# Two-dimensional neighbourhood attention layer: query blocks paired anew so that four bias tables serve in place of six, the final root by logarithm and exponential on ACT, and the last head pair of every row group split without a round trip through memory

## The chip, the cores and the metric

The kernel runs on one core of one Trainium2 chip. A core has five engines with queues of their own: TensorE (PE, matrix products, with PEld for its weight loads), VectorE (DVE), ScalarE (ACT), GpSimd (POOL) and SyncE (SP, which here issues nearly all DMAs). The metric is the time of one execution in microseconds (us), less is better; several runs are taken and their median is compared.

## What is computed

One layer over 2048 tokens of 1024 features, laid out as a grid of 32 rows by 64 columns, all in float32. A root-mean-square norm, a projection to q, k, v and a gate (4 x 1024 columns), attention with 16 heads of 64 features, an output projection with the input added, and a final norm:

```python
h = rmsnorm(x, norm_0)
q, k, v, gate = split(h @ w_in_0, 4)
# query (r, c): keys in a window of 8 rows by 16 columns, moved inward at the border
s = q . k * 64 ** -0.5 + rpb[head, kr - r + 7, kc - c + 15]      # outside the window: -1e30
o = softmax(s) @ v
x = x + (o * silu(gate)) @ w_out_0
return rmsnorm(x, norm_f)            # x * rsqrt(mean(x * x) + 1e-6) * norm_f
```

## The kernel before

**Three stages.** `stage_one` and `stage_two` do the projections, for each half of the tokens, by a scheme of seven products of half-size blocks, each in three float32r products of high and low parts (h·h, h·l, l·h; `split_to` makes the parts: ACT copies to the rounded type, DVE subtracts). Their results q, k, v and the gate go to memory. The third stage, the loop over `m` at L1281, does the attention and, between its pieces, the rest of the value projection (`values_left`, 192 matmuls) and then the output projection (`outputs`, 768 matmuls); these matmuls are called the fill here.

**Attention steps.** `order` has 32 steps: four row groups T of eight grid rows, and in each eight head pairs p. A step has 512 queries, by columns eight strips of 8 columns by 8 rows, that is 64 queries a strip. A strip sees the keys of three strips, its own and the two beside it, over 11, 15, 15 or 12 key rows by row group. Two strips share the 128 partitions of a block; a block C in 0 to 3 held strips 2C and 2C+1.

- `scores` (L916): q times k into PSUM (line 929, tile s), then DVE adds the table `EM` and takes the minimum over a row (L937), and ACT makes the exponential with its sum (L943). Tables hold the bias and -1e30 outside the window, so they depend on the row group, the head, and on where the block stands: first, middle (blocks 1 and 2) or last, so three kinds by two heads, six tables. `load_tab` (L902) loads them for a step, into two buffers `em`.
- `normalise` (L946): DVE takes the reciprocal of the four sums of half a step (L948), and POOL multiplies the four tiles (L952). The second half of a step is normalised in the next turn of the loop.
- `turns` (L954): TensorE transposes the weights, strip by strip, into PSUM (ph, L968); ACT copies those of the lower 64 partitions and DVE those of the upper 64 to SBUF (pta, L971), in three rounds.
- `values` (L974): the weights times v (o, L986), times the gate (DVE, og, L990). The result goes to memory (`keep`, L992), to be loaded by row tiles of 128 tokens (`load_og`).

**The output part.** There are 16 row tiles n, four in a row group; tile n needs all eight head pairs of its row group, 128 columns (a slot) each. `load_og` loads the slots (ograw, L1043), `split_og` makes the high and low parts (ACT L1056 gh, DVE L1057 gl), and 24 matmuls for each half j of the columns (L1210, L1212, L1214, tile po) make a turn. `turns_` lists the turns. In row groups 0 and 3 the last head pair's result is also split directly (`direct`, L997, into the tile `last`), so that the first two row tiles of these groups load only seven slots; `parts`, `whole` and `og_ready` say what must be there. `add_rows` adds the input (DVE, L1089) and squares with a sum (ACT, L1092). `finish` queues the root: eight small DVE instructions (L1106 to L1113, a first guess from the bits and two steps of refinement), then the scaling (`scale`, L1121, two of 128x512 on DVE), then the store (`send`, L1125). For the last tile the root is a square root on ACT (L1103), whose activation table is loaded by an early square root (L1081), and a reciprocal on DVE.

**What sets the order.** The order is written by hand. All is issued in program order on each engine. `clock` counts the matmuls of the fill; `store` keeps a piece of work until the clock has reached a due time (`due`). `now` is the clock with 26 added for each step. A turn of the loop is: `feed(10)` (ten matmuls), `normalise` of the second half of the step before, then four portions of fill, each with a `split_rows` or a load of weights (`consume`) ahead of it, `run_roots` behind the second portion, the last 0.3 of the amount (with up to `calm_debt` = 6 matmuls in advance where something was added or split within 8 counts), then `turns`, `scores` of the next step with the first half's `normalise` in it, and `values`. About 24 matmuls of fill stand in a step. `split_rows` splits a tile that was loaded 40 counts ago, whole, and at most three turns away. A root is run at the earliest 8 counts behind its tile's last addition; its scaling comes 9 counts behind the root and its store 27. SP issues the DMAs of a step in this order: the store of og, then v, q, the table, the keys, the gate, with row tiles, inputs, weights and stores of output in between.

## Time and profile before

| | before |
|---|---|
| median of 3 runs | 1052.13 us (1048.69 to 1052.44) |
| the profiled execution, its own time | 1049.58 us |
| its span | 1047.8 us |
| granted TensorE clock | 0.998 |
| busy: PE, PEld, DVE, ACT, POOL | 1033.4, 819.7, 706.6, 482.2, 214.4 us |
| DMA | 200.25 MB, mean 191 GB/s |
| the attention stage, from its first fill to the last matmul | 598.7 to 1041.6 us |

The span is what the profile covers, from its first to its last instruction. PE's busy time is modelled and includes short waits. Rows of groups give the line, the engine, the operation, out<-in with shapes, the count, then busy us, mean ns of one, idle us ahead and what ended it. Rows of the timeline and of the chain begin with the start and the length in us. In brackets stands the idle time ahead of an instruction and what ended it.

### The profile page before, as it was taken

How to read it: one execution, taken by the hardware profiler on the slowest of the kernel's cores; microseconds unless marked ns; L12 is line 12 of the kernel's file. 1: busy time of each engine (PE TensorE's matmuls, PEld its weight loads, DVE VectorE, ACT ScalarE, POOL GpSimd, SP SyncE). 2: the span in 40 equal slices, each digit the busy share in tenths (PEclk: the TensorE clock that was granted, in tenths of full speed). 3: DMA queues.
4: the chain of work that ended last, by engine and by line, in shares of the span. 5: the costliest groups of instructions: out<-in, count | busy, mean ns of one | idle time of the engine just before them, and what ended most of it. 6: DMA issues, size and time to landing. Idle time of an engine off the chain costs nothing.

```text
span 1047.8 us, 19452 instructions
## 1 busy us (share of the span) xinstructions
PE 1033.4 (99%) x7024; PEld 819.7 (78%) x7024; DVE 706.6 (67%) x1596; ACT 482.2 (46%) x1176; POOL 214.4 (20%) x321
## 2 busy tenths in 40 slices
PE   9999999999999999999999999999999999999997
PEld 6888888887888878888888777777776777677786
DVE  5476657768897885656565756668687778777544
ACT  7645323234333352323232356676555555556422
POOL 0000231321321400000000024345333333333200
PEclk9999999999999999999999999999999999999999
DMA  9633444452634432423324798999879788977442
GB/s 320 222 101 110 140 149 126 130 151 99 193 124 148 120 121 81 140 102 121 112 90 138 224 276 257 332 321 321 276 254 325 268 287 272 318 247 266 132 151 80
DMA packets 113336, 200.25 MB, mean 191 GB/s; under 512 B 10008, under 2 KB 44184, under 8 KB 111192
## 3 DMA queue, kind: packets, MB, share of 16 engines
q1 hardware_dynamic: 112808, 198.61, 58.4%
q8 instruction: 55, 0.90, 0.3%
q10 hardware_dynamic: 432, 0.40, 0.1%
q14 instruction: 41, 0.34, 0.1%
HBM read 148.64 MB, written 50.33 MB: 190 GB/s over the span
## 4 chain that ended last, share of the span: by engine, by line
PE 86%; DVE 6%; DMA 3%; ACT 2%; issue 2%; SPq 1%; POOL 0%; DVEq 0%; POOLq 0%; ACTq 0%
PE pp L356 41%; PE pv L480 8%; PE s L929 7%; PE o L986 7%; PE po L1210 5%; PE po L1214 5%; PE po L1212 5%; PE ph L968 4%; PE pv L849 4%; DMA ograw<-ogd 1%; DVE l L439 1%; DMA kt<-kd 1%; ACT x L943 1%; DMA qt<-qd 1%; DVE land L434 1%
## 5 line engine op out<-in xcount | busy, mean ns | idle before, releaser
L356 PE MATMUL pp<-h,f 128*128 128x512 f32 x768 | 248.6, 389 | 0.0
L952 POOL TENSOR_SCALAR x<-x,st 128x360 f32<-128x360 f32 (+2 forms) x256 | 142.0, 573 | 257.8 <-DVE st L948 243.9
L356 PEld LDWEIGHTS pp<-h,f 128*128 128x128 f32 x768 | 144.2, 188 | 30.6
L356 PE MATMUL pp<-four,f 128*128 128x512 f32 x648 | 161.7, 391 | 0.5 <-DVE u L369 0.4
L943 ACT ACTIVATE x<-x,st 128x360 f32<-128x360 f32 (+2 forms) x256 | 139.8, 547 | 33.5 <-DVE st L937 33.5
L356 PE MATMUL pp<-l,f 128*128 128x512 f32 x384 | 149.7, 390 | 0.0
L356 PEld LDWEIGHTS pp<-four,f 128*128 128x128 f32 x648 | 121.3, 188 | 27.2 <-DVE u L369 1.5
L376 POOL TENSOR_TENSOR tmp<-tmp,rb 128x512 f32<-128x512 f32 x36 | 59.2, 1646 | 268.9 <-DVE tmp L374 224.1
L937 DVE CUSTOM_DVE_ANT_0 x<-s,em 128x360 f32<-128x360 f32 (+2 forms) x256 | 108.7, 480 | 2.9 <-PE s L929 1.7
L1210 PE MATMUL po<-woh,gh 128*128 128x512 f32 x248 | 98.4, 397 | 1.0 <-ACT gh L1056 1.0
L1212 PE MATMUL po<-woh,gl 128*128 128x512 f32 x248 | 97.6, 393 | 1.4 <-DVE gl L1057 1.4
L1214 PE MATMUL po<-wol,gh 128*128 128x512 f32 x248 | 97.5, 393 | 0.0
L971 DVE COPY pta<-ph 120x512 f32<-120x512 f32 (+5 forms) x96 | 56.0, 637 | 51.8 <-PE ph L968 51.8
L986 PEld LDWEIGHTS o<-pta,vt 120*64 120x64 f32 (+2 forms) x1024 | 68.5, 137 | 22.8 <-DVE st L937 15.2
L929 PE MATMUL s<-kt,qt 64*64 64x360 f32 (+2 forms) x1024 | 83.8, 439 | 2.2 <-DMA kt<-kd 1.2
L971 ACT ACTIVATE pta<-ph 120x512 f32<-120x512 f32 (+5 forms) x96 | 47.0, 557 | 81.7 <-PE ph L968 81.7
L356 PEld LDWEIGHTS pp<-l,f 128*128 128x128 f32 x384 | 72.1, 188 | 15.1
L986 PE MATMUL o<-pta,vt 120*64 120x192 f32 (+5 forms) x1024 | 83.4, 316 | 0.0
L439 DVE TENSOR_TENSOR f<-raw,f 128x512 fp32r<-128x512 f32 x80 | 55.1, 691 | 28.2 <-ACT f L438 28.2
L364 ACT ACTIVATE p<-pp 128x512 f32<-128x512 f32 x24 | 14.4, 598 | 123.2 <-PE pp L356 123.2
L374 DVE TENSOR_TENSOR tmp<-pp,u 128x512 f32<-128x512 f32 x48 | 33.1, 690 | 47.5 <-PE pp L356 42.9
L438 ACT ACTIVATE f<-raw 128x512 fp32r<-128x512 f32 x80 | 49.3, 625 | 33.1 <-PE pp L356 12.5
(160 smaller groups left out, 1635.7 us busy)
## 6 DMA issues: line engine op xcount, KB each, us to landing
raw<-in_wg_dram SPq DMA_DIRECT2D x124, 256.0 KB, 4.5
em<-in_tab_dram SPq DMA_DIRECT2D x16, 1080.0 KB, 7.7
vd<-v SPq DMA_DIRECT2D x32, 256.0 KB, 2.9
sgd<-sg SPq DMA_DIRECT2D x32, 256.0 KB, 2.9
qt<-qd SPq DMA_DIRECT2D x32, 256.0 KB, 5.4
sgt<-sgd SPq DMA_DIRECT2D x32, 256.0 KB, 9.4
ogd<-og SPq DMA_DIRECT2D x32, 256.0 KB, 2.9
xr<-in_x_dram SPq DMA_DIRECT2D x32, 256.0 KB, 7.3
```

What stands on the lines that cost most here:

```text
L356: nc.tensor.matmul(B[n, P], t[:, int(m == 2), c], x[k][int(m == 1)], start=P in (1, 6, 5) and k == 0 and m == 0, stop=k == 3 and m == 2, s ...
L439: nc.vector.tensor_tensor(l, t, h.bitcast(F32), OP.subtract)
L480: nc.tensor.matmul(ps[t], a[:, o], b, start=k == 0 and m == 0, stop=k == NK - 1 and m == 2)
L929: nc.tensor.matmul(pst[s][h * 64:h * 64 + 64], qt[a, C * 128 + h * 64:C * 128 + h * 64 + 64], keys.rearrange("p r (s c) -> p s r c", c=8), ...
L937: nc.vector.tensor_tensor_reduce(X[i, C][s], pst[s], EM[p, T, COL_TYPE[C], s], -1.0, 1e38, OP.add, OP.min, st[:, o:o + 1])
L943: nc.scalar.activation(X[i, C][s], X[i, C][s], AF.Exp, bias=st[:, o:o + 1], scale=-1.0, accum_out=st[:, 4 + o:5 + o])
L952: nc.gpsimd.tensor_scalar(X[i, C][s], X[i, C][s], st[:, o:o + 1], 1.0, op0=OP.mult, op1=OP.mult)
L971: (nc.vector.tensor_copy if h else lambda o, i_: nc.scalar.activation(o, i_, AF.Copy))(to[:k, :, 2 - j, c, h], at[h][:k, :, c])
L986: nc.tensor.matmul(o[s * 64:s * 64 + 64, g0 * 64:g1 * 64 + 64].rearrange("d (g q) -> d g q", q=64), vt[:k, strip, s * 64:s * 64 + 64], t[: ...
L1210: nc.tensor.matmul(p, gh, woh[q, j], start=(i == 0), stop=False)
L1212: nc.tensor.matmul(p, gl, woh[q, j], start=False, stop=False)
L1214: nc.tensor.matmul(p, gh, wol[q, j], start=False, stop=(i == NK - 1))
```

## The change

- **Blocks.** Block C now holds the strips `BLOCKS[C]`: (0, 7), (1, 4), (2, 5), (3, 6). The first block has the two border strips, the other three have only middle strips, so there are two kinds of table by two heads, four tables. `scores`, `turns` and `bias_tables` follow; the flat order of the transposed weights stays by strip.
- **Direct split.** `direct` and the seven-slot loads are done in all four row groups.
- **Roots.** For every tile the sum of squares goes through a logarithm and an exponential with scale -0.5 on ACT; for all but the last one DVE instruction adds the two halves first. The activation table that has both functions is loaded ahead of the attention loop, by name. The gain is scaled accordingly and the last tile's product has no constant any more.
- **Order.** `run_roots` stands behind `normalise` at the head of a turn of the loop; the scaling comes 6 counts behind the root and the store 24. `split_rows` splits a second tile in the same step only if it is at most one turn away. `calm_debt` is 4.

```diff
-COL_TYPE = [0, 1, 1, 2]
+BLOCKS = [(0, 7), (1, 4), (2, 5), (3, 6)]
-TAB_AT = [6 * sum(TYPE_N[:t]) for t in range(4)]
+TAB_AT = [4 * sum(TYPE_N[:t]) for t in range(4)]
...
-            t = emp([128, 2160], F32, "em")[:, :6 * n]
-            for c in range(6):
+            t = emp([128, 1440], F32, "em")[:, :4 * n]
+            for c in range(4):
                 EM[p, T, c // 2, c % 2] = t[:, c * n:c * n + n]
-            nc.sync.dma_start(t, tab[p, :, TAB_AT[ty]:TAB_AT[ty] + 6 * n])
+            nc.sync.dma_start(t, tab[p, :, TAB_AT[ty]:TAB_AT[ty] + 4 * n])
...
-                at = EDGE + (2 * C + h - 1) * 8
+                b = BLOCKS[C][h]
+                at = EDGE + (b - 1) * 8
...
-        to = t.rearrange("p (s j c h q) -> p s j c h q", s=2, j=3, c=4, h=2)
+        to = t.rearrange("p (s j h c q) -> p s j h c q", s=2, j=3, c=4, h=2)
...
-            cs = [[C for C in range(4) if 0 <= 2 * C + h - 1 + j < 8] for h in range(2)]
+            cs = [[c for c in range(4) if 0 <= 4 * h + c - 1 + j < 8] for h in range(2)]
...
-                    to[:k, :, 2 - j, c, h], at[h][:k, :, c])
+                    to[:k, :, 2 - j, h, c], at[h][:k, :, c])
...
-        if T in (0, 3) and p == lastp[T]:
+        if p == lastp[T]:
             store(("last", T), 2, direct)
...
-        return NK - 1 if T in (0, 3) and i < 2 else NK
+        return NK - 1 if i < 2 else NK
...
-                nc.scalar.activation(st[:, 7:8], st[:, 6:7], AF.Sqrt)
...
-            nc.vector.scalar_tensor_tensor(w, y, 0.5 ** 0.5 / NF_SCALE, late["nf"][j], op0=OP.mult, op1=OP.mult)
+            nc.vector.tensor_tensor(w, y, late["nf"][j], OP.mult)
...
             if n == tiles - 1:
-                nc.scalar.activation(h, st[:, 5:6], AF.Sqrt, bias=st[:, 7:8], scale=1.0)
-                nc.vector.reciprocal(r, h)
-                return
-            nc.vector.tensor_scalar(h, st[:, 0:1], st[:, 1:2], 0.5 * D * EPS, op0=OP.add, op1=OP.add)
...
-            nc.vector.scalar_tensor_tensor(r, a, 5 / ROOT_K ** 2, r, op0=OP.add, op1=OP.mult)
+                nc.scalar.activation(h, st[:, 5:6], AF.Ln, bias=st[:, 7:8], scale=1.0)
+            else:
+                nc.vector.tensor_scalar(a, st[:, 0:1], st[:, 1:2], 0.5 * D * EPS, op0=OP.add, op1=OP.add)
+                nc.scalar.activation(h, a, AF.Ln)
+            nc.scalar.activation(r, h, AF.Exp, scale=-0.5)
...
-            store(("y", n), 9, scale)
-            store(("y", n), 27, send)
+            store(("y", n), 6, scale)
+            store(("y", n), 24, send)
...
-        if n < ready["loaded"] and "turn" in ready and place[n] <= ready["turn"] + 3 and now() - late["loaded_at"][n] >= 40 and whole(n) \
+        if n < ready["loaded"] and "turn" in ready and place[n] <= ready["turn"] + (1 if split_run[0] == runs[0] else 3) and now() - late["loaded_at"][n] >= 40 and whole(n) \
...
+            split_run[0] = runs[0]
...
-    calm_debt = 6
+    calm_debt = 4
...
+    nc.scalar.preload_act_table_set("natural_log_exp_and_others")
     for m in range(cycles + 1):
...
             normalise(2 * m - 1)
+        run_roots()
         middle(m)
...
-                if k == 1:
-                    run_roots()
```

More of the change, by code (lines that the diff above doesn't have):

```diff
@@ L25 @@
 EPS = 1e-6
-ROOT = (0.703952253, 2.38924456)
-ROOT_K = 2 * (2 * ROOT[0]) ** 2
-NF_SCALE = -2 * ROOT[0] * 0.375 * ROOT_K ** 2
 NEG = -1e30
@@ L48, in bias_tables @@
         r0, r1 = KEY_ROWS[T]
-        for C in (0, 1, 3):
+        for C in (0, 1):
             half, qr, col, strip, kr, kc = np.ogrid[:2, T * 8:T * 8 + 8, :8, :3, r0:r1, :8]
-            qc = C * 16 + half * 8 + col
-            kc = C * 16 + half * 8 + (strip - 1) * 8 + kc
+            block = np.array(BLOCKS[C])[half]
+            qc = block * 8 + col
+            kc = (block + strip - 1) * 8 + kc
             rs = np.clip(qr - KH // 2, 0, ROWS - KH)
@@ L928, in scores @@
                     keys = kt[a, at:at + r * GW].rearrange("p (r c) -> p r c", c=GW)[:, :, :24]
-                    nc.tensor.matmul(pst[s][h * 64:h * 64 + 64], qt[a, C * 128 + h * 64:C * 128 + h * 64 + 64],
+                    nc.tensor.matmul(pst[s][h * 64:h * 64 + 64], qt[a, b * 64:b * 64 + 64],
                                      keys.rearrange("p r (s c) -> p s r c", c=8), start=True, stop=True)
@@ L936, in scores @@
                 o = 2 * j + s
-                nc.vector.tensor_tensor_reduce(X[i, C][s], pst[s], EM[p, T, COL_TYPE[C], s], -1.0, 1e38,
+                nc.vector.tensor_tensor_reduce(X[i, C][s], pst[s], EM[p, T, int(C > 0), s], -1.0, 1e38,
                                                OP.add, OP.min, st[:, o:o + 1])
@@ L961, in turns @@
             at = [x.rearrange("p (s c q) -> p s c q", s=2, c=4) for x in b]
-            cs = [[C for C in range(4) if 0 <= 2 * C + h - 1 + j < 8] for h in range(2)]
+            cs = [[c for c in range(4) if 0 <= 4 * h + c - 1 + j < 8] for h in range(2)]
             for s in range(2):
                 for C in range(4):
-                    for h in range(2):
-                        if C in cs[h]:
+                    for h, g in enumerate(BLOCKS[C]):
+                        if g % 4 in cs[h]:
                             q = slice(64 * h, 64 * h + 64)
-                            nc.tensor.transpose(at[h][:k, s, C], X[2 * m + C // 2, C][s][q, j * k:j * k + k], ident[q, q])
+                            nc.tensor.transpose(at[h][:k, s, g % 4], X[2 * m + C // 2, C][s][q, j * k:j * k + k], ident[q, q])
             for h in range(2):
@@ L1013, in late_loads @@
                                                ap=[[0, 128], [1, 512]]))
-            store(("nf", j), 40, lambda j=j: nc.scalar.activation(accs[j], accs[j], AF.Copy, scale=float(D) ** 0.5 * NF_SCALE))
+            store(("nf", j), 40, lambda j=j: nc.scalar.activation(accs[j], accs[j], AF.Copy, scale=(0.5 * D) ** 0.5))
         late["nf"] = accs
@@ L1162, in split_first @@
             ready["split"] += 1
+    split_run = [-1]
     def split_rows():
         n = ready["split"]
-        if n < ready["loaded"] and "turn" in ready and place[n] <= ready["turn"] + 3 and now() - late["loaded_at"][n] >= 40 and whole(n) \
+        if n < ready["loaded"] and "turn" in ready and place[n] <= ready["turn"] + (1 if split_run[0] == runs[0] else 3) and now() - late["loaded_at"][n] >= 40 and whole(n) \
                 and sum(1 if len(g) == 2 else 2 for g in G.values()) <= 6:
```

6 lines of the change are left out of this document (removed).

## The prediction

> **What bounds the kernel now.** I read the head of the page first, then the chain of waits, then the waits of TensorE alone, then the timeline around each of them. All numbers are of the profiled execution: span 1047.8 us, its own time 1049.58 us, so 1.8 us lie outside the span. The three runs have a median of 1052.13 us, 2.55 above this execution, and a lowest of 1048.69, 0.89 below.
>
> ```profile
> span 1047.8 us, 19452 instructions
> PE 1033.4 (99%) x7024; PEld 819.7 (78%) x7024; DVE 706.6 (67%) x1596; ACT 482.2 (46%) x1176; POOL 214.4 (20%) x321
> ```
>
> TensorE is the bound. The diff changes no matmul shape and no count: the transposes stay 44 a step (three, four and four of four places for one half of the partitions, four, four and three for the other, as before), and the value products read the same flat layout, since strip block 2C+h and the new 4h+c both run from 0 to 7 in order. So only time in which TensorE waits can go, and a busy share of 99% hides some of it because the ends of matmuls are modelled. I therefore read the lengths of the attention steps from the chain of waits: each step starts with the transposes (ph), and columns are start, length, what.
>
> ```profile
> 771.80 1.43 PE ph L968 x35
> 773.23 3.11 PE s L929 x32
> ...
> 812.12 1.43 PE ph L968 x34
> 813.54 2.58 PE s L929 x32
> ...
> 824.35 1.59 PE ph L968 x42
> ...
> 837.88 1.43 PE ph L968 x31
> ...
> 850.11 1.59 PE ph L968 x41
> ...
> 863.65 1.43 PE ph L968 x33
> ...
> 927.11 1.36 PE ph L968 x44
> ...
> 938.94 1.36 PE ph L968 x44
> ...
> 951.00 1.36 PE ph L968 x44
> ```
>
> An undisturbed step of the two middle row groups lasts 12.23 us (812.12 to 824.35, and 837.88 to 850.11). Steps in which a square root of a finished row tile and a split of another run on VectorE last 13.53 and 13.54: 1.3 too long, twice. From 771.80 to 812.12 three steps take 40.32, which is 3.63 over three of 12.23; in each of the three the scores take about 3.11 instead of 2.58 (0.53), 1.6 in all, and the other 2.0 are the change of row group, below. In the last group a step with a root takes 12.06 and one without 11.83, 0.23 apart.
>
> What TensorE itself waits for, outside those steps (columns: total us, times, longest):
>
> ```profile
> PE po L1212 <- DVE gl L1057: 1.4, 2, 1.1
> ...
> PE s L929 <- DMA kt<-kd: 1.2, 1, 1.2
> PE po L1210 <- ACT gh L1056: 1.0, 1, 1.0
> ```
>
> **Part 1: four bias tables for six.** Each load of em shrinks by a third: 1080 KB become 720, 792 become 528. VectorE's and ACT's work per block stays, since every block still has its own add-and-minimum and exponential.
>
> ```profile
> em<-in_tab_dram SPq DMA_DIRECT2D x16, 1080.0 KB, 7.7
> ...
> em<-in_tab_dram SPq DMA_DIRECT2D x8, 792.0 KB, 6.6
> ```
>
> ```profile
> 658.51 8.87 DMA kt<-kd
> ...
> 665.53 1.75 DVE L971 COPY pta<-ph 88x512 f32<-88x512 f32 x3 [2.12 <-PE ph L968]
> ```
>
> These loads are hidden but for one place: the keys of the seventh step, queued on SP behind em and three smaller loads, land 8.87 us after their issue and TensorE waits 1.2 for them (the kt row above). The table ahead of them is 264 KB smaller. At the 792 KB in 6.6 us of its own row that is 2.2 us less to move, more than the wait. Late next are the copies of the transposes, which VectorE ends at 667.28 and which free the banks of the later scores, so I take **-1.0**; bounds 0 (it is the issue, not the bytes) and -1.2.
>
> **Part 2: the last head pair split directly in every row group.** The first row tiles of groups 1 and 2 (tiles 4 and 8) now load seven of eight slots, so the load need not wait until the last pair was stored. Before, it was issued at 797.17 and landed 9.82 later, and only then could ACT begin the split that the waiting product reads:
>
> ```profile
> 797.17 9.82 DMA ograw<-ogd
> 807.01 0.64 ACT gh L1056
> ```
>
> With the seventh pair's store as condition it goes out a step, some 12 us, earlier; the 40-count wait in `split_rows` (26 for a step, 24 for its matmuls) is then just met in the following step, after the direct split has filled the eighth slot. So both waits go: 1.0 + 1.4 = 2.4 by idle time, 3.4 (2.0 + 1.4) by lengths of steps. I take **-2.9**. What is added is one ACT copy and one VectorE subtraction for each of two groups:
>
> ```profile
> L1001 DVE TENSOR_TENSOR last<-og,last 128x256 fp32r<-128x256 f32 x2 | 0.8, 420 | 0.7 <-ACT last L1000 0.7
> ...
> L1000 ACT ACTIVATE last<-og 128x256 fp32r<-128x256 f32 x2 | 0.8, 408 | 4.1 <-DVE og L990 4.1
> ```
>
> They stand ahead of the reciprocal for which POOL waits; POOL ends 0.16 before the transposes begin (below), so up to 0.42 twice may show. With the smaller shifts (the debt of 4 for 6 moves two matmuls between steps, one split a step, other due times) I book **+0.4**; bounds -0.5 and +1.
>
> **Part 3: the root on ACT, earlier in the step.** Removed are eight VectorE instructions a row tile (the first and the last of the eight, for the eleven tiles before the end), added are one sum on VectorE, in the form of L1106, and a logarithm and an exponential of 128x1 on ACT.
>
> ```profile
> L1106 DVE TENSOR_SCALAR st<-st 128x1 f32<-128x1 f32 x11 | 2.2, 201 | 2.8 <-ACT xr L1092 2.8
> ...
> L1113 DVE SCALAR_TENSOR_TENSOR st<-st 128x1 f32<-128x1 f32 x11 | 1.8, 159 | 0.4
> ```
>
> A plain step with a root, by the timeline (start, length, engine, line):
>
> ```profile
> 794.59 0.17 DVE L948 RECIPROCAL st<-st 128x4 f32<-128x4 f32 x1
> 794.67 0.18 DVE L1106 TENSOR_SCALAR st<-st 128x1 f32<-128x1 f32 x1
> ...
> 794.93 2.19 POOL L952 TENSOR_SCALAR x<-x,st 128x360 f32<-128x360 f32 x4 [1.82 <-DVE st L1106]
> ...
> 797.28 1.50 PE L968 MATMUL ph<-ident,x 64*120 64x64 f32 x44
> 797.35 1.41 DVE L1121 SCALAR_TENSOR_TENSOR y<-y,st,acc 128x512 f32<-128x512 f32 x2
> ...
> 798.68 1.75 DVE L971 COPY pta<-ph 120x512 f32<-120x512 f32 x3
> ```
>
> The root holds VectorE from 794.67 to 797.35, the scaling (L1121) until 798.7, and the copies of the transposes come behind it; that is the 0.53. Afterwards the sum ends at 794.85. The nearest row for logarithm and exponential is the square root of the last tile, 0.29:
>
> ```profile
> 1037.71 1.28 ACT L1081 ACT_TABLE_LOAD   x1
> ...
> 1043.09 0.29 ACT L1103 ACTIVATE st<-st 128x1 f32<-128x1 f32 x1
> ```
>
> Two of them and two crossings between engines give a root about 1 us after the reciprocal of 794.59 (estimate), and the scaling, now 6 counts behind instead of 9 and issued from the tenth matmul instead of the fifteenth, runs from about 795.7 to 797.1. VectorE is then free for the copies. But there it meets POOL, which scales the last blocks from 794.93 to 797.12, 0.16 before the transposes begin. What wide VectorE work does to POOL:
>
> ```profile
> 706.99 2.18 DVE L167 TENSOR_TENSOR wol<-raw,woh 128x512 fp32r<-128x512 f32 x3 [0.16 <-ACT woh L166]
> 707.02 3.67 POOL L952 TENSOR_SCALAR x<-x,st 128x360 f32<-128x360 f32 x4 [1.75 <-ACT woh L166]
> ...
> 708.52 0.44 PE L968 MATMUL ph<-ident,x 64*120 64x64 f32 x5
> ...
> 710.21 1.75 PE L968 MATMUL ph<-ident,x 64*120 64x64 f32 x39 [1.24 <-POOL x L952]
> ...
> 711.88 1.44 PE L929 MATMUL s<-kt,qt 64*64 64x360 f32 x16
> ```
>
> Beside 2.18 us of subtraction the same four POOL instructions took 3.67 instead of 2.19, 1.48 more, or 0.68 for each us. So 1.42 of scaling costs POOL between 0.96 (that share) and 1.42 (all of it). POOL then ends 0.8 to 1.26 late; in the rows above POOL ended 2.17 after the transposes' start (710.69 against 708.52), and the scores began 3.36 after it instead of 1.43, 1.93 lost: 0.24 is absorbed, because the first blocks can go ahead. So I book 0.6 for a plain step with a root, against 0.53 saved: nothing won there. In the two steps with a split ACT's copy of it now queues behind the logarithm, which waits for VectorE's sum; subtraction and scaling then follow each other until about the copies, and I expect 0.5 too long instead of 1.3, 0.8 won twice. The last group wins its 0.23 in two or three steps. Together 3 x 0.07 - 1.6 - 0.6 = **-2.0**; bounds: -5 (1.6 + 2.6 + some 0.8, all of it) and +2 (rival 1).
>
> The load of the activation table (1.28) goes from the end, where it lay under the last matmuls, to the start of the attention part, where ACT idles 2.12 before its first exponential:
>
> ```profile
> 603.06 0.52 ACT L943 ACTIVATE x<-x,st 128x264 f32<-128x264 f32 x1 [2.12 <-DVE st L937]
> ```
>
> Nothing at either place; without that cover 1.28. In the last tile a square root on ACT (0.29) and a reciprocal on VectorE become two ACT instructions in a row: 0, with bounds of 0.3, one such instruction, either way. Everything else (the multiplication by the final gain without a constant) keeps its form.
>
> **Sum.** 1049.58 - 1.0 - 2.9 + 0.4 - 2.0 = 1044.1. The runs before lay from 0.89 below to 2.86 above the profiled one; I add 0.6, less than their median did, because a transfer that came late is one likely reason for the long ones and there is less to transfer: **1044.7 us**.
>
> **The rivals.**
>
> 1. *The scaling shuts POOL out.* If a wide VectorE instruction stops POOL for its whole length, a plain root step costs 1.42 - 0.16 - 0.24 = 1.0 instead of 0.53 (three times), one with a split 0.3 more than now (twice): +2 instead of -2, 1049.58 - 1.0 - 2.9 + 0.4 + 2 + 0.6 = 1048.7, no change that counts. For it: 3.67 against 2.19. Against: POOL lost 0.68 of each us there, not all. The Trainium skill (SBUF — State Buffer, Who interferes with whom) says that a VectorE instruction with two SBUF inputs and a GpSimd one that reads SBUF exclude each other for a whole instruction. By that rule this rival comes out.
> 2. *All of the relief.* POOL is done before the scaling starts, or what it loses is covered: 1049.58 - 1.2 - 3.4 - 5 + 0.6 = 1040.6. For it: the last group's steps, where a root cost only 0.23. Against: the 0.16 of 797.12 and 797.28.
> 3. *Slower: ACT changes tables at each root.* If the logarithm and the exponential of the scores don't stay in one loaded table, each root pays two loads of 1.28. The root is then 2.6 later and the scaling falls on the copies; it decides from about 1.0 of lateness (scaling end 797.1, copies due near 798.0). Eleven roots times (2.6 - 1.0) = 17.6 in place of the 5 or so of now: 1049.58 - 3.9 + 12.5 + 0.6 = 1058.8. For it: the square root needed a load of its own (1037.71). Against: one load is asked for by name before the loop. The Trainium skill (ScalarE: Activation LUTs, Table sets: the hidden batching unit) lists exponential and logarithm together in that named set, and puts a switch at about 2.7 us; by that, two switches a root would come to about 5.3 us of ACT, an estimate from the page. The 1.28 of the row above shows the load alone.
> 4. *It doesn't do what it says.* The split of tile 4 misses its step by the 40-count wait, and the keys are late by their issue, so only part 3 and the small shifts stay: 1049.58 - 2.0 + 0.4 + 0.6 = 1048.6. For it: the 40 counts are met by some 4 only. Against: the loads before went out as soon as they could (797.17).
>
> **How the numbers follow.** Forecast 0.48 (own range 1041.5 to 1047.5), rival 1 0.24, rival 2 0.14, rival 3 0.08, rival 4 0.06. Faster by over 0.5% (about what a measurement tells from no change) is under 1046.9: nearly all of the forecast, rival 2 and a little of 1, 0.63. Slower by over 0.5%, over 1057.4, is rival 3 and accidents, 0.08. The rest 0.29. The range, 1039.5 to 1050, leaves out rival 3 and the outer half of rival 2.
>
> **What would show it.** No wait of po for gl or gh at the change of group; no wait of s for kt; no table load after the one ahead of the loop; steps with a root at 12.2 to 12.8 with the scaling inside POOL's stretch and POOL's four instructions at 3.1 to 3.6 (rival 1: steps over 13; rival 2: 12.23). The copies of the transposes no longer wait behind the scaling. I am wrong if TensorE gains a new wait for ACT behind the logarithm, or if the step at 708.52, which nothing here mends, grows.

## The result, and the profile after

| | before | after |
|---|---|---|
| median of 5 runs | 1049.10 us (1048.64 to 1052.44) | 1040.18 us (1039.69 to 1044.62) |
| the profiled execution, its own time | 1049.58 us | 1039.84 us |
| ahead of the attention (start of its first fill matmul) | 598.51 | 597.03 |
| attention (from there to the start of the last matmul) | 442.71 | 434.15 |
| behind it, to the end of the span | 6.58 | 6.87 |
| DMA | 200.25 MB | 189.57 MB |

The ratio is 0.9912, with a 95% interval from 0.9885 to 0.9940: 0.9% faster. The recorded time was 1044.7, so the direction was right and the size was not: 1040.18 is 4.5 us lower, next to the 1040.6 of the rival "all of the relief". It lies inside the recorded range (1039.5 to 1050) and below the forecast's own (1041.5 to 1047.5).

The three stretches add up to the spans, 1047.80 and 1038.05. Of the 9.74 us between the profiled executions 8.56 lie in the attention. The projections ahead of it were 1.48 shorter, though of their work only the one table that is loaded there differs, and with it the places of data in memory. Their time has two parts. Up to the start of the 101st matmul (26.98 before, 26.82 after) it differs from execution to execution: 26.7 to 28.2 in the fourteen profiles of this document, 27.18 and 28.21 in the two of one and the same kernel. From there to the attention the three kernels that load six tables' bytes (the one before and two of the experiments) take 571.49 to 571.53, and the eleven that load four 570.18 to 570.30, all at a granted clock of 0.998 or 0.999. So 1.3 of the 1.48 goes with the smaller tables; by what means is not shown. Kernels are compared by the attention stretch below, which leaves this 1.3 out.

The head of the page after, and then the waits of TensorE after (columns: total us, times, longest):

```profile
span 1038.1 us, 19333 instructions
...
PE 1026.9 (99%) x7024; PEld 817.6 (79%) x7024; DVE 684.9 (66%) x1492; ACT 488.1 (47%) x1208; POOL 221.6 (21%) x321
```

```profile
PE ph L967 <- POOL x L951: 2.6, 5, 0.8
```

TensorE's 7024 matmuls are the same, and VectorE has 104 instructions fewer. The waits of po for gl and gh and the wait of s for kt are gone, as foreseen (the last for a second reason too, see the first experiment). What is left in the attention is the first row: the transposes wait for POOL. The tables moved a third less, by the DMA row after:

```profile
em<-in_tab_dram SPq DMA_DIRECT2D x16, 720.0 KB, 6.6
```

A step with a root and no split, by the timeline after:

```profile
764.22 0.69 DVE L1087 TENSOR_TENSOR y<-po,xr 128x512 f32<-128x512 f32 x1 [1.57 <-PE po L1209]
764.83 0.17 DVE L947 RECIPROCAL st<-st 128x4 f32<-128x4 f32 x1
764.92 0.18 DVE L1103 TENSOR_SCALAR st<-st 128x1 f32<-128x1 f32 x1
765.13 0.20 ACT L1104 ACTIVATE st<-st 128x1 f32<-128x1 f32 x1 [2.12 <-DVE st L1103]
765.17 3.14 POOL L951 TENSOR_SCALAR x<-x,st 128x360 f32<-128x360 f32 x4 [1.89 <-DVE st L1103]
765.37 0.20 ACT L1105 ACTIVATE st<-st 128x1 f32<-128x1 f32 x1
765.60 1.72 DVE L1113 SCALAR_TENSOR_TENSOR y<-y,st,acc 128x512 f32<-128x512 f32 x2 [0.51 <-ACT st L1105]
...
767.52 2.05 PE L967 MATMUL ph<-ident,x 64*120 64x64 f32 x44
```

The root now ends 0.65 us behind the start of the sum (764.92), and the scaling lies from 765.60 to 767.32, inside POOL's stretch. POOL takes 3.14 instead of the 2.19 of before, and the transposes 2.05 instead of 1.50.

The wide rows of POOL and of the scaling hold four and two instructions. One by one they read:

```profile
765.17 0.57 POOL L951 TENSOR_SCALAR x<-x,st 128x360 f32<-128x360 f32 x1 [1.89 <-DVE st L1103]
765.60 0.75 DVE L1113 SCALAR_TENSOR_TENSOR y<-y,st,acc 128x512 f32<-128x512 f32 x1 [0.51 <-ACT st L1105]
765.71 1.08 POOL L951 TENSOR_SCALAR x<-x,st 128x360 f32<-128x360 f32 x1
766.27 1.05 DVE L1113 SCALAR_TENSOR_TENSOR y<-y,st,acc 128x512 f32<-128x512 f32 x1
766.77 0.99 POOL L951 TENSOR_SCALAR x<-x,st 128x360 f32<-128x360 f32 x1
```

They take turns. The second POOL instruction ends 0.44 behind the end of the first scaling (766.79 against 766.35), the second scaling 0.53 behind the end of that one, and the third POOL instruction 0.44 behind the end of the second scaling. So the one that starts second waits until the other has ended, and then needs 0.44 or 0.53 more, less than its undisturbed 0.57 or 0.75. (Only the first scaling, started 0.14 ahead of the end of the first POOL instruction, shows no wait.) POOL loses 0.51 and 0.42 in this way, the second scaling 0.3.

The chain of waits after, around a step with a root and a split:

```profile
831.71 1.43 PE ph L967 x44
...
841.82 3.05 POOL x L951 x3
844.91 1.21 PE ph L967 x32
...
856.91 1.43 PE ph L967 x44
```

From 831.71 to 856.91 two steps take 25.20. With 12.23 for the undisturbed one the other lasts 12.97 (13.54 before). POOL itself now stands in the chain; before it was the copies of the transposes, on VectorE.

### The profile page after: what moved, and what is told of

Its sections match the earlier page's. It is cut to its first block, busy times and chain, and to the rows that moved or that the text cites. A ratio compares the mean times of both kernels' runs of the same rounds, so it can differ in the third digit from the quotient of the medians.

```text
span 1038.1 us, 19333 instructions
## 1 busy us (share of the span) xinstructions
PE 1026.9 (99%) x7024; PEld 817.6 (79%) x7024; DVE 684.9 (66%) x1492; ACT 488.1 (47%) x1208; POOL 221.6 (21%) x321
## 2 busy tenths in 40 slices
DMA packets 113336, 189.57 MB, mean 183 GB/s; under 512 B 10008, under 2 KB 44184, under 8 KB 113240
## 4 chain that ended last, share of the span: by engine, by line
PE 88%; DVE 6%; POOL 2%; issue 2%; ACT 1%; DMA 0%; POOLq 0%; DVEq 0%; ACTq 0%
PE pp L354 41%; PE pv L478 9%; PE o L985 7%; PE s L928 7%; PE po L1205 5%; PE po L1209 5%; PE po L1207 5%; PE ph L967 4%; PE pv L847 4%; POOL x L951 2%; DVE l L437 1%; ACT x L942 1%; DVE land L432 1%; ACT h L436 0%; DVE land L791 0%
## 5 line engine op out<-in xcount | busy, mean ns | idle before, releaser
L951 POOL TENSOR_SCALAR x<-x,st 128x360 f32<-128x360 f32 (+2 forms) x256 | 149.1, 602 | 242.3 <-DVE st L947 222.1
L1205 PE MATMUL po<-woh,gh 128*128 128x512 f32 x240 | 95.0, 396 | 0.0
L1209 PE MATMUL po<-wol,gh 128*128 128x512 f32 x240 | 94.3, 393 | 0.0
L1207 PE MATMUL po<-woh,gl 128*128 128x512 f32 x240 | 94.1, 392 | 0.0
L928 PE MATMUL s<-kt,qt 64*64 64x360 f32 (+2 forms) x1024 | 78.7, 437 | 0.0
```

What stands on the lines that cost most here:

```text
L928: nc.tensor.matmul(pst[s][h * 64:h * 64 + 64], qt[a, b * 64:b * 64 + 64], keys.rearrange("p r (s c) -> p s r c", c=8), start=True, stop=True)
L951: nc.gpsimd.tensor_scalar(X[i, C][s], X[i, C][s], st[:, o:o + 1], 1.0, op0=OP.mult, op1=OP.mult)
L1205: nc.tensor.matmul(p, gh, woh[q, j], start=(i == 0), stop=False)
L1207: nc.tensor.matmul(p, gl, woh[q, j], start=False, stop=False)
L1209: nc.tensor.matmul(p, gh, wol[q, j], start=False, stop=(i == NK - 1))
```

## The experiments

Unless said otherwise a kernel is the kernel after with one edit, seen in one profiled execution, and its attention stretch is set against 434.15. In the table, "transposes", "scores" and "fill" say where the difference lies, as the sums of these pieces over the stage. Turn m is counted here from its transposes to those of turn m + 1: it has the transposes of one step, the scores of the next, the values, and the fill that follows. The scores of the seventh step, of which the prediction speaks, stand in turn 6, and the changes of row group that matter in turns 17 and 25.

| | own time | attention | difference | transposes | scores | fill |
|---|---|---|---|---|---|---|
| six tables' bytes again | 1043.88 | 436.71 | +2.6 | -0.1 | +2.3 | +0.4 |
| no direct split in groups 1, 2 | 1043.31 | 436.79 | +2.6 | -0.4 | +0.1 | +3.0 |
| old root, old place | 1042.78 | 435.96 | +1.8 | -3.2 | +5.0 | 0 |
| normalise after 6 matmuls | 1035.17 | 429.15 | -5.0 | -4.3 | -0.7 | 0 |
| ACT root, old place | 1039.77 | 433.99 | -0.2 | +0.7 | -0.9 | 0 |
| VectorE root, new place | 1042.53 | 436.93 | +2.8 | -3.9 | +6.6 | 0 |
| old debt, old rule of splits | 1043.15 | 436.69 | +2.5 | +1.0 | +1.6 | 0 |
| old debt alone | 1041.21 | 434.72 | +0.6 | +0.5 | 0 | +0.1 |
| table not asked for by name | 1045.83 | 436.88 | +2.7 | -3.9 | +6.6 | -0.1 |

Two kernels are the one before with one edit, set against its 442.71:

| | own time | attention | difference | transposes | scores | fill |
|---|---|---|---|---|---|---|
| pairing alone | 1043.67 | 438.03 | -4.7 | -1.3 | -2.4 | -1.0 |
| normalise after 6 matmuls alone | 1043.53 | 436.86 | -5.9 | -2.5 | -3.7 | +0.3 |

**The bytes of the tables.** Six columns are loaded, four are used.

```diff
-        for C in (0, 1):
+        for C in (0, 1, 1):
...
-            nc.sync.dma_start(t, tab[p, :, TAB_AT[ty]:TAB_AT[ty] + 4 * n])
+            nc.sync.dma_start(t, tab[p, :, TAB_AT[ty]:TAB_AT[ty] + 6 * n])
```

> The changed kernel, but each table load moves six tables' worth of bytes again (two tables are loaded twice and the second copy is not used). If the smaller tables ended the wait of the scores for the keys in the seventh step, that wait is back with 1.0 to 1.7 us, and nothing else moves by more than 0.5: the profiled execution comes out 1 to 2 us over the changed kernel's 1039.84. Rival: the wait went because other loads were issued in another order; then no wait of s for kt appears and the time stays within 0.5.

The keys of the seventh step were in time, so here the first part of the rival holds: the order of the issues had changed. The timeline of SP's issues in this kernel:

```profile
654.38 0.42 SPq L908 DMA_DIRECT2D em<-in_tab_dram  x1
654.89 0.38 SPq L875 DMA_DIRECT2D kt<-kd  x1
```

The keys are issued 0.51 behind the table and ahead of the two loads of the final gain. In the kernel before they stood behind those two, 3.54 after the table (658.51 against 654.97), and with the old debt of six in the kernel after they do so again (3.03). So the smaller debt brings the keys in time even behind the larger table. The rival's second part, a time within 0.5, did not come out: the loss came at another place, in the scores of turn 9, 1.9 longer. The chain of waits of this kernel there:

```profile
695.77 0.06 ACT gh L1055
...
696.29 0.51 ACT gh L1055
696.79 0.39 ACT pta L970
...
697.22 0.35 PE s L928
```

ACT's split of the first row tile waits for its load. The load was issued 2.68 behind the keys of its step instead of 1.22, and its last packet ended at 695.01, 0.4 behind the start of the transposes; in the kernel after it ended 1.8 ahead of them. The copies of the transposes queue behind the split on ACT, and the scores wait for their banks. So the bytes are worth some 2.6 us of the attention in this kernel, and the 1.3 ahead of it, not by one fixed wait but by whichever load is the last in time. The scores of the outer row groups stayed as short as in the kernel after, which matters below.

**The direct split.** Groups 1 and 2 take the round trip through memory again.

```diff
-        if p == lastp[T]:
+        if T in (0, 3) and p == lastp[T]:
...
-        return NK - 1 if i < 2 else NK
+        return NK - 1 if T in (0, 3) and i < 2 else NK
```

> The changed kernel, but the last head pair is split directly only in row groups 0 and 3, as before. If the direct split ended the two waits at the change of row group, po waits again for gh and gl, 1.7 and 1.4 us by the lengths of the fill stretches, about 3.2 in all. Rival: those waits went because tiles are split one a step and the roots have left VectorE; then both stretches stay under 0.5 us over their matmuls.

The fill of turns 17 and 25 grew by 1.45 and 1.47, and among the waits of TensorE stands

```profile
PE po L1207 <- DVE gl L1056: 2.3, 2, 1.1
```

The transposes of these two turns are 0.34 and 0.27 shorter without the direct split, which therefore has a small price there.

**The root: engine and place.** Three kernels: both put back, then ACT's root at the old place (behind the second portion of the fill, scaling 9 counts later), then VectorE's eight instructions at the new place. The edit of the place, and that of the engine cut to its core:

```diff
-        run_roots()
         middle(m)
...
+                if k == 1:
+                    run_roots()
...
-                nc.scalar.activation(h, a, AF.Ln)
-            nc.scalar.activation(r, h, AF.Exp, scale=-0.5)
+            nc.vector.scalar_tensor_tensor(a, r, h, r, op0=OP.mult, op1=OP.mult)
```

> The changed kernel with the root of before: eight VectorE instructions, run behind the second portion of fill, scaling 9 and store 27 counts later, and a square root for the last tile. By the lengths of steps the scores of root steps then wait 0.5 to 1.2 us for the copies again and the transposes' waits for POOL of 0.5 to 0.9 vanish: plain root steps of the middle groups the same within 0.1, those with a split 0.55 longer each, the last row group 1.0 to 1.6 longer, together 2 to 3 us over 1039.84. Rival 1 of the prediction (POOL shut out) would have it shorter than the changed kernel.

> The changed kernel with its root on ACT, but run where it was before: behind the second portion of fill, scaling 9 and store 27 counts later. If the place decides (the scaling must neither meet POOL nor the copies), the scaling falls on the copies again and the scores of root steps wait 0.4 to 0.6 us for them, less than with the eight VectorE instructions since 2 us of VectorE are free ahead of it; POOL is left alone: within 1 us of the changed kernel's attention part. If the engine decides, the waits of the scores are gone as well and it is 3 us shorter than the changed kernel.

> The changed kernel with the eight VectorE instructions of before in the new place, directly behind the second half's reciprocals, scaling 6 counts later. Narrow instructions don't hold POOL up (2.19 us beside 2.0 us of them in the kernel before), but they push the scaling some 2 us later, past most of POOL's stretch and into the copies: transposes wait under 0.4 us, scores 0.5 to 1.2 us in root steps, total 1 to 3 us over the changed kernel's attention part. If it is the place alone that counts, it equals the changed kernel within 0.5.

Putting back both costs 1.8, a little less than the 2 to 3 expected. ACT's root at the old place costs nothing, VectorE's root at the new place costs 2.8. So the engine decides, not the place. The expectation that at the old place the scaling would fall on the copies again was wrong; the timeline of that kernel in a plain root step shows it inside POOL's stretch as before:

```profile
765.07 3.05 POOL L951 TENSOR_SCALAR x<-x,st 128x360 f32<-128x360 f32 x4 [1.90 <-DVE st L1103]
...
765.93 1.75 DVE L1113 SCALAR_TENSOR_TENSOR y<-y,st,acc 128x512 f32<-128x512 f32 x2 [0.93 <-ACT st L1105]
```

VectorE idles at that time (0.93 ahead of the scaling), so a scaling issued some matmuls later starts only 0.4 later within POOL's work. With the root on VectorE the waits change sides: the transposes win 3.9 and the scores lose 6.6, waiting for the copies that VectorE makes behind root and scaling:

```profile
PE s L931 <- DVE pta L973: 3.1, 6, 0.9
```

In the new place 30 of the 40 small root instructions with a second input tensor that run beside POOL take 0.4 to 0.51 instead of 0.16 to 0.22. Each of them ends together with a POOL instruction, as the rows of the kernel before show further below.

**Normalisation earlier.** If the transposes wait for POOL because the scaling runs beside it, starting POOL earlier should take that wait away.

```diff
-        feed(10)
+        feed(6)
         if m:
             normalise(2 * m - 1)
+        feed(4)
         run_roots()
```

> The changed kernel, but the second half's normalise is issued after six matmuls of fill instead of ten, so that VectorE's reciprocal does not stand behind the addition of a row tile; the roots stay behind the tenth. If the transposes wait in root steps because POOL's four products and the scaling of a finished tile meet, POOL is now done before the scaling starts: its four instructions take about 2.2 instead of 3.1 to 3.6 us, the transposes 1.43 instead of 2.0 to 2.3, and 3 to 4 us go (1036 to 1037). Rival: POOL is not what the transposes wait for, or the reciprocal waits for ACT's sums instead; then less than 0.5 changes.

> The kernel after with the second half's normalisation issued after six of a step's ten fill matmuls in place of all ten, nothing else, timed against the kernel before. One profiled look gave 1035.17 against 1039.84 of the kernel after, 4.7 less, of which 5.0 lie in the attention steps (the transposes' waits for POOL: 4.3). If these are the cost of the root's scaling meeting POOL, as the theory has it, the median is 1034.7 to 1036.2, 0.4 to 0.5% under the kernel after (1040.18) and 1.3 to 1.4% under the kernel before (1049.1). If the one look was a fast pace of the projections (0.25% between profiled executions), the median is above 1038.

The first of the two, seen once, won 5.0 in the attention, more than the 3 to 4 expected. Timed, the kernel's median is 1035.86 (1034.44 to 1036.31), and the ratio to the kernel before (1049.86 in these runs) is 0.9859, with an interval from 0.9838 to 0.9880. It beats both kernels; the kernel after had 0.9912 (0.9885 to 0.9940). The transposes of all root steps are back at 1.43, or 1.36 in the last group. Its attention took 428.85, 5.3 less than after: 4.3 of it in turns with a root, 0.7 in turn 10, which has a split of weights and no root, and 0.2 in turn 4. The timeline of its profile ahead of the transposes of turn 17, where a root and a split meet:

```profile
788.64 0.17 DVE L947 RECIPROCAL st<-st 128x4 f32<-128x4 f32 x1
...
789.00 2.20 POOL L951 TENSOR_SCALAR x<-x,st 128x360 f32<-128x360 f32 x4 [0.79 <-DVE st L947]
...
789.15 0.69 DVE L1087 TENSOR_TENSOR y<-po,xr 128x512 f32<-128x512 f32 x1 [0.35 <-PE po L1209]
...
792.13 1.40 DVE L1113 SCALAR_TENSOR_TENSOR y<-y,st,acc 128x512 f32<-128x512 f32 x2
...
792.45 1.50 PE L967 MATMUL ph<-ident,x 64*120 64x64 f32 x44
```

The reciprocal now stands ahead of the addition to y, which waits for TensorE's product. POOL is done at 791.20, before the scaling, and neither stretches the other: 2.20 and 1.40.

**The same in the kernel before.**

> The kernel before with only the second half's normalisation moved up to the sixth of a step's ten fill matmuls; tables, direct split, root and order as before. Theory: in the kernel before, the scaling of a root step comes after POOL's four instructions and falls on the copies of the transposes, so moving the normalisation up brings the root and the scaling forward by nothing (they are issued by their own counts) and wins only what POOL costs now: the late transposes of the steps beside the splits of weights and of the tenth step (0.8 to 1.4 each), 1 to 2.5 in all over the attention steps, 440.2 to 441.7. Rival: the early normalisation is worth about as much alone as in the kernel after (5.0), because VectorE's queue is freed earlier whatever the root's engine: 437.7 or less.

The theory fell: 5.9 are won here too, more than the rival's 5.0. Of these, 3.7 lie in turns with a root and 2.1 in turns 5, 6, 9 and 10, which have none; in turn 6 the wait for the keys is gone, and why it went was not followed up. Two timelines around the transposes of turn 17. The kernel before, then this one:

```profile
793.98 0.69 DVE L1089 TENSOR_TENSOR y<-po,xr 128x512 f32<-128x512 f32 x1 [1.58 <-PE po L1214]
794.59 0.17 DVE L948 RECIPROCAL st<-st 128x4 f32<-128x4 f32 x1
...
795.47 0.57 POOL L952 TENSOR_SCALAR x<-x,st 128x360 f32<-128x360 f32 x1
795.53 0.51 DVE L1110 SCALAR_TENSOR_TENSOR st<-st 128x1 f32<-128x1 f32 x1
```

```profile
789.41 0.18 DVE L948 RECIPROCAL st<-st 128x4 f32<-128x4 f32 x1 [0.40 <-ACT x L943]
790.59 0.69 DVE L1089 TENSOR_TENSOR y<-po,xr 128x512 f32<-128x512 f32 x1 [1.00 <-PE po L1214]
791.20 0.20 DVE L1106 TENSOR_SCALAR st<-st 128x1 f32<-128x1 f32 x1
...
792.07 0.16 DVE L1110 SCALAR_TENSOR_TENSOR st<-st 128x1 f32<-128x1 f32 x1
...
792.91 1.41 DVE L1121 SCALAR_TENSOR_TENSOR y<-y,st,acc 128x512 f32<-128x512 f32 x2
...
794.62 1.75 DVE L971 COPY pta<-ph 120x512 f32<-120x512 f32 x3 [0.30 <-PE ph L968]
```

In the kernel before, the reciprocal had to stand behind an addition that idled 1.58 for a product, so POOL and the root started at the same time. The small root instruction of the last row then ended together with the POOL instruction that ran when it started (both at 796.04). So did all 33 of its kind that started beside POOL in this kernel: each ended within 0.01 us of the end of that POOL instruction. With POOL gone ahead the eight root instructions take 1.7 (791.20 to 792.91) instead of the 2.7 of before (794.67 to 797.35), the scaling is over before the copies, and no wait of the scores is left in a plain root step.

**The order of debt and splits.**

```diff
-place[n] <= ready["turn"] + (1 if split_run[0] == runs[0] else 3)
+place[n] <= ready["turn"] + 3
...
-    calm_debt = 4
+    calm_debt = 6
```

> The changed kernel with a fill debt of 6 instead of 4 and two tiles to be split in one step as before. The prediction booked +0.4 for these smaller shifts. If they are neutral, the attention part stays within 0.5 us of the changed kernel's 434.2 (first fill to last matmul). Rival: they carry part of the gain that parts 1 to 3 leave open (about 1.5 us): the step at 705 and the scores of the first and last row group get longer again, 1 to 2 us.

> The kernel after with the debt of six fill matmuls in place of four, nothing else; one split a step stays. Undoing both together cost 2.57 in the attention steps, 1.66 of it where two tiles were split in one step of the last group. Theory: the order of the splits carries it, so the debt alone costs 0 to 0.9 (attention 434.2 to 435.0) and no step of the last group grows by over 0.5. Rival: the debt carries it, because two matmuls moved between steps change when the second split is issued: 2 to 2.6 (436.2 to 436.8).

Both together cost 2.5, so these shifts are not neutral; the debt alone costs 0.6, as the theory of the last run had it. The 2.0 between the two lie in turn 25, whose scores take 3.79 instead of 2.52, and in turn 17, whose transposes and scores are 0.4 and 0.35 longer. The timeline of the first of the two kernels ahead of the scores of turn 25:

```profile
892.90 1.03 ACT L1055 ACTIVATE gh<-ograw 128x512 fp32r<-128x512 f32 x2
...
894.45 1.03 ACT L1055 ACTIVATE gh<-ograw 128x512 fp32r<-128x512 f32 x2
895.09 1.39 DVE L1056 TENSOR_TENSOR gl<-ograw,gh 128x512 fp32r<-128x512 f32 x2 [0.39 <-ACT gh L1055]
...
896.40 1.40 DVE L1113 SCALAR_TENSOR_TENSOR y<-y,st,acc 128x512 f32<-128x512 f32 x2
...
897.73 1.74 DVE L970 COPY pta<-ph 96x512 f32<-96x512 f32 x3
898.46 0.20 PEld L928 LDWEIGHTS s<-kt,qt 64*64 64x64 f32 x6 [1.04 <-DVE pta L970]
```

The direct split makes tiles ready earlier, and by the old rule two are then split in one step. The second split delays the subtraction, that the scaling, that the copies. In the kernel before, two tiles were split in one step as well, behind the transposes of turn 17, and the scores of turn 18 took the 2.58 of an undisturbed step. So the new rule is worth 2 us in the kernel after, where it keeps what the direct split would else give back; what it does without the direct split was not tried.

**The table.** The load by name is left out.

```diff
-    nc.scalar.preload_act_table_set("natural_log_exp_and_others")
```

> The changed kernel without the load of the table that has both functions. This is rival 3 of the prediction put to the test: if the logarithm and the exponential are then served from two tables, some 30 loads of 1.28 us appear on ACT, two a root; the root comes 2.6 us later and each of the eleven root steps before the end grows by 1 to 1.7 us, 10 to 18 us in all (1050 to 1058). If one table is loaded at the first logarithm and stays, there is one load more and the time is the changed kernel's within 1.

The groups by line of this kernel show a load ahead of each logarithm and each exponential of a root (the last tile's logarithm, on another line, has one more):

```profile
L1105 ACT ACT_TABLE_LOAD x16 | 20.5, 1283 | 0.3
L1104 ACT ACT_TABLE_LOAD x15 | 19.2, 1283 | 0.3
```

So the danger of rival 3 is real, and the one line prevents it. Its price was smaller than forecast: 2.7 in the attention, where the later root frees POOL from the scaling (3.9 won) and the scaling falls on the copies (6.6 lost), and 2.3 behind it (9.13 against 6.87 from the last matmul to the end).

**The pairing alone.**

> The kernel before with only the first and last query block paired, so four tables for six; direct split, root, debt and order as before. Theory: the wait of the seventh step for its keys (1.2 before) goes, and that step's transposes, which began late for it, lose their 1.7 too only if they were late through the same wait: 1.2 to 1.7 less in the attention steps than the kernel before (442.7), so 441.0 to 441.5, with the waits for gl and gh of tiles 4 and 8 still there (2.4). Rival: undoing the pairing in the kernel after cost 2.4 through another load, that of the first split tile; if that load was already late in the kernel before, 2.4 and more is won here: 440.3 or less. The smaller rival, that the loads are late by their issue and not by their bytes: 442.5 to 442.9.

It won 4.7, more than the theory and the rival allowed. The seventh step gives 1.3, as the theory had it: with the old order of the issues the smaller tables bring the keys in time. Turn 9, with the first split tile, gives only 0.2, so the rival's reason is not it. The rest: the scores are 0.09 to 0.17 shorter in 20 of the 31 turns, 2.4 in all, and the fill 1.0, of which 0.3 at a change of row group, where the loads of the row tiles land earlier. The scores of turn 2 in the kernel before and then in this one, with VectorE's copies that free their banks:

```profile
624.05 1.75 DVE L971 COPY pta<-ph 88x512 f32<-88x512 f32 x3 [3.08 <-PE ph L968]
...
624.72 2.25 PE L929 MATMUL s<-kt,qt 64*64 64x264 f32 x32
```

```profile
622.66 1.75 DVE L973 COPY pta<-ph 88x512 f32<-88x512 f32 x3 [2.93 <-PE ph L970]
...
623.33 2.16 PE L931 MATMUL s<-kt,qt 64*64 64x264 f32 x32
```

The copies start equally far ahead of the scores (0.67) and last as long, and the scores still take 0.09 less. The kernel with six tables' bytes and the new pairing had these short scores too, so it is the pairing and not the bytes. Where it came from inside the 32 matmuls stays open: the third block's matmuls are held once in the kernel before where they run through after, but why their banks or weights come in another order was not tried.

## Why the prediction was right and wrong

The sum, term by term. "Measured" is from the steps: the pairing by its own kernel, the rest by the turns in which the kernel after differs from the one with the pairing alone.

| term | booked | measured |
|---|---|---|
| part 1, four tables | -1.0 | -4.7 |
| part 2, direct split | -2.9 | -2.9 (turn 17 -1.4, turn 25 -1.5) |
| smaller shifts | +0.4 | -0.5 (turn 4 +0.3, turn 6 -0.4, turn 10 -0.4) |
| part 3, root | -2.0 | -0.5 |
| ahead of the attention | 0 | -1.5 |
| behind it | 0 | +0.3 |
| all | -5.5 | -9.8, where the two executions show -9.7 |

By this table the forecast is 4.3 short: part 1 was booked 3.7 too small, the smaller shifts 0.9 too dear and the 1.5 ahead of the attention at nothing. Against this part 3 was booked 1.5 too large. That the time came to lie inside the range is luck to this extent: with part 3 as booked it would have been 1038.7, below the range.

**Part 1 is the step that failed.** "These loads are hidden but for one place" held for the wait that it named: 1.3 won in the seventh step by the pairing alone, 1.0 booked. In the kernel after, the order of the issues ends this wait already, and there the bytes save another, in turn 9. The lower bound of -1.2 took the loads for the whole of the part, and so missed most of it. The pairing also changes the order in which blocks are made and their banks are used, and that shortened the scores of most steps by 0.1 to 0.2. The prediction had seen only that counts and the flat layout stay. A part that reorders every step needs a bound for every step: 31 times 0.1 is more than all that was booked here. The 1.3 that the smaller tables save ahead of the attention was not thought of either.

**Part 2** came out as booked by the lengths of steps; the idle time of the waits alone (2.4) would have been too little. Leaving the direct split out again cost 2.6.

**The smaller shifts** were taken for a cost of +0.4 (bounds -0.5 and +1). They came out at the lower bound. Above all, the rule of one split a step was worth 2 us beside the direct split: without it parts 2 and 3 would have lost that in turns 25 (1.3) and 17 (0.75). What falls due in one step when tiles are ready earlier was not asked.

**Part 3.** For the plain root step the two sizes were right: 0.6 booked for the transposes and 0.55 measured (2.05 against 1.50), 0.53 booked for the scores and 0.53 to 0.56 measured. But 0.13 to 0.16 of the latter are the pairing's, so that the root itself lost 0.15 there. POOL lost 0.95 (3.14 against 2.19) for 1.42 of scaling, the lower of the two bounds, 0.96, which decided against the price of rival 1. By the Trainium skill (SBUF — State Buffer, Who interferes with whom) the two engines exclude each other for a whole instruction, and by that rule rival 1 was to come out. The single records agree with the rule, since each waits for the other's end, but not with the price: POOL waited 0.64 and 0.55 for the two scalings and needed 0.13 less each time afterwards. That a share of 0.68 gave the right sum is therefore luck in part.

Two things were worse than booked. The steps with a root and a split won 0.57 each (13.54 to 12.97) where 0.8 was booked, 0.17 of it through the pairing. And turn 17 lost some 0.5 (transposes 0.9 longer, scores 0.4 shorter) where next to nothing was booked, 0.3 of it since the direct split has put a split beside its root. In sum: the three steps booked as plain came to +0.8 for the +0.2 booked, the two with a split -0.8 for -1.6, the last group -0.6 as booked, and +0.1 elsewhere. Of the signs that were named, the plain root steps last 12.78 and 12.77, inside 12.2 to 12.8; the two with a split, 12.97 and 12.99, lie above. Undone in the finished kernel part 3 is worth 1.8, more than the -0.5 of the table; the parts are not independent, and their undoings (2.6, 2.6, 1.8 and 2.5) add up to 9.5 where 8.6 were measured.

What part 3 did not see is why the root collides with anything. The prediction took the reciprocal's start at 794.59 as given. It stood behind an addition that idled for a product. That one place in VectorE's queue set POOL, the root and the scaling against each other in both kernels, and the exclusion made each of them wait for the others. Putting the reciprocal four matmuls earlier was worth 5.9 before and 5.0 to 5.3 after in the attention, more than any part of the change, of which 3.7 and 4.3 lie in turns with a root.

**The rivals.** All of the relief gave nearly the right number for wrong reasons: its 5 for the roots were not there. The switch of tables does happen without the named load, at 5.0 over the kernel after (2.7 + 2.3) where the expectation of that run had 10 to 18, since a later root also stops stretching POOL. The split of tile 4 and the keys met their steps, so "it doesn't do what it says" fell.

**The rest.** The 0.6 for the distance between profiled execution and median was about right (0.34 after). Of the 1.5 ahead of the attention 1.3 goes with the smaller tables, as the fourteen profiles show, and 0.2 is the start of one execution.

## What to carry to other kernels

When an edit reorders work inside every step, bound it per step and multiply by the steps; a list of the waits that go is not the sum. When two engines collide, look first at what held the earlier of them: an instruction whose inputs are ready may stand behind one that waits for another engine, and moving it ahead cost at most 0.3 of fill here. A row of the timeline that merges several instructions hides who waits for whom; single records show it. Whatever makes work ready earlier also makes more of it ready at once, so a limit per step belongs to the same change.

## What the runs showed of the hardware

- Where a VectorE instruction with two input tensors and one of POOL's met in the rows above, the one that waited ended a fixed time behind the end of the other: the 128x1 root instructions within 0.01 us of it (33 of 33 in the kernel before; 0.51 for three of the four beside POOL in turn 17, 0.16 to 0.22 with POOL gone ahead), the scaling of 128x512 0.53 and POOL's 128x360 0.44 behind it. By the sums of such waits POOL's four took 3.14 instead of 2.19 and the scaling 1.72 instead of 1.42 after the change.
- A load of the activation table took 1.28 in each of the 31 cases of the rows above, with 0.3 us of idle time ahead of a whole group together. The Trainium skill (ScalarE: Activation LUTs, Table sets: the hidden batching unit) puts a switch at about 2.7; no row here shows more than the 1.28.
- At a granted clock of 0.998 to 0.999 the start of the 101st matmul varied from 26.7 to 28.2 between executions. From there to the attention kernels with the same size of tables agreed within 0.12 us, and those with six tables' bytes took 1.3 us longer than those with four.
